# Block products: which of two accumulators is copied out before the third sum

## The chip, the cores and the metric

The kernel runs on one core of a Trainium2 chip. What counts is the device time of one execution, in microseconds (us). Of the kernel before, three runs gave 2841.8, 5434.66 and 2838.23 us, so the median is 2841.8 us. TensorE is called PE below (PEld is its weight load), VectorE is DVE, ScalarE is ACT, GpSimd is POOL and SyncE is SP.

## The reference

One transformer block over 2048 rows of width 1024, in float32: an RMSNorm and one input projection, two groups of attention heads, an output projection with a residual add, a second RMSNorm and a gated FFN of width 2816, and a last norm. The change touches only the products in the first and the last of these stages:

```python
h = rmsnorm(x, norm1_g[l])
proj = jnp.einsum('bsd,de->bse', h, w_in[l])
dq, dk, dv, fq, fk, fv, fg = jnp.split(proj, SPLITS, axis=-1)
...
h2 = rmsnorm(x, norm2_g[l])
g = jnp.einsum('bsd,df->bsf', h2, w_gate[l])
u = jnp.einsum('bsd,df->bsf', h2, w_up[l])
x = x + jnp.einsum('bsf,fd->bsd', jax.nn.silu(g) * u, w_down[l])
```

## The kernel before

The large matrix products are cut into two by two blocks and computed with seven block products (P1 to P7) in place of eight, as Strassen and Winograd do it. In the input projection the class `Features` does this for a pair of 128 output features, in the FFN the class `Matrix` does it for one gate or one up matrix (11 of each for each half of the rows, so 44 matrices; in the trace each of them has three matmul lines, L1393 to L1395, and those of `Features` have L434 to L436). One product is twelve matmuls of 128x128 by 128x512: four slices of the inner dimension, and for each slice three matmuls, because every float32 operand is split into a high part (a cast on ACT, L159) and a low part (a subtraction on DVE, L160).

The products of one matrix are computed in the order P1, P2, P6, P5, P7, P3, P4. They go to three banks of PSUM: A takes P1, then P6, P7 and P4 are accumulated on top; B takes P5 and then P3; C takes P2. After a product its method `take` reads the bank. With (i, j) for the four output blocks this gives

- (0, 0): a copy of A after P1 (ACT), plus C after P2 (DVE, L1408 or L449)
- (0, 1): a copy of A after P6 (ACT), plus B after P3 (DVE, L1411 or L452)
- (1, 1): a copy of A after P7 (ACT, L1403 or L444), plus B, which then holds P5 alone (DVE, L1405 or L446)
- (1, 0): A after P4, read where it lies

A product that accumulates on a bank cannot start before the readers of that bank are done. So P3 (bank B) waits for the DVE sum of (1, 1), and P4 (bank A) waits for the ACT copy after P7. In the FFN `done` then applies the silu (ACT, L1422) or multiplies gate by up (DVE, L1426), and `activations` forms sums of the results (DVE, L1440 to L1448) in a ring of three buffers named t, which POOL stores to DRAM (a_d, L1435). In the first half of the rows the same ring and DVE also make the sums of blocks of w_down (L1346, reading tiles wd, stored as wd_d by POOL, L1461).

A scheduler of the framework sets the order of the instructions on each engine from its own cost model. Each engine then runs its list strictly in that order. Beside the products, the first part of the input projection also loads further rows of x (SP, L209), squares them (ACT, L217), forms the reciprocal root (POOL, L218 and L137 to L138), scales the rows (ACT, L221), and transposes them (PE, L246). The later part computes the forget gates (ACT L709 to L711 with table loads, a DVE scan in L716).

Of the kernel before, what the change touches and what calls it, by code (L numbers as in the profile page):

```python
# [59 lines left out]
def block_kernel(  # L60
# [21 lines left out]
    nc = tc.nc  # L82
# [79 lines left out]
    with ExitStack() as c1:  # L162
# [32 lines left out]
        def ut(name="u"):  # L195
            return up.tile([P, 512], F32, name=name, tag="u")
# [194 lines left out]
        class Features:  # L391
# [46 lines left out]
            def take(self, p):  # L438

                acc, d = self.bank[BANK_OF[p]], self.dst  # L440
                if p in ("P1", "P6", "P7"):
                    i = dict(P1=(0, 0), P6=(0, 1), P7=(1, 1))[p]
                    d[i] = ut()
                    nc.scalar.copy(d[i], acc)  # L444
                    if p == "P7":
                        nc.vector.tensor_add(d[1, 1], self.bank["B"], d[1, 1])  # L446
                        self.done(1, 1)
                elif p == "P2":
                    nc.vector.tensor_add(d[0, 0], acc, d[0, 0])  # L449
                    self.done(0, 0)  # L450
                elif p == "P3":
                    nc.vector.tensor_add(d[0, 1], acc, d[0, 1])  # L452
                    self.done(0, 1)
                elif p == "P4":
                    d[1, 0] = acc
                    self.done(1, 0)
# [864 lines left out]
    with ExitStack() as c4:  # L1321
# [9 lines left out]
        def t2(ring, name):  # L1331
            return rings[ring].tile([P, 512], F32, name=name, tag=ring)
# [25 lines left out]
        class Matrix:  # L1358
# [38 lines left out]
            def take(self, p):  # L1397

                acc, d = self.bank[BANK_OF[p]], self.dst
                if p in ("P1", "P6", "P7"):  # L1400
                    i = dict(P1=(0, 0), P6=(0, 1), P7=(1, 1))[p]
                    d[i] = t2("u" if self.up else "g", "u")
                    nc.scalar.copy(d[i], acc)  # L1403
                    if p == "P7":
                        nc.vector.tensor_add(d[1, 1], self.bank["B"], d[1, 1])  # L1405
                        self.done(1, 1)
                elif p == "P2":
                    nc.vector.tensor_add(d[0, 0], acc, d[0, 0])  # L1408
                    self.done(0, 0)
                elif p == "P3":  # L1410
                    nc.vector.tensor_add(d[0, 1], acc, d[0, 1])  # L1411
                    self.done(0, 1)
                elif p == "P4":
                    d[1, 0] = acc
                    self.done(1, 0)
# [351 lines left out]
```

## Time and profile before

| | |
|---|---|
| median of three runs | 2841.8 us |
| the profiled execution, and its span | 2842.74 us, 2840.9 us |
| PE busy in the span | 2753.1 us, 97% |
| DVE, ACT, POOL busy | 1910.0 us, 1502.0 us, 629.8 us |
| granted clock from 1546 to 1995 us, FFN's first half | 1.00 |
| granted clock from 93 to 200 us, input projection | 0.90 |

The span is the profiled execution from its first to its last instruction. A matmul of 512 columns is shown with 0.39 us although the next one starts some 0.23 us later: matmuls overlap in the pipeline, and so a stall of PE is best read from the starts of two neighbours, not from the idle time alone. The granted clock is the share of 2.4 GHz that TensorE was given.

### The profile page before, as it was taken

To read this page: it belongs to the slowest core of one execution; us is meant where nothing else is said; L and a number is where in the kernel's file an instruction comes from. 1 tells how busy PE (TensorE), PEld (TensorE's weight loads), DVE (VectorE), ACT (ScalarE), POOL (GpSimd) and SP (SyncE) were. 2 spreads that over 40 slices of the span, in tenths; PEclk is the share of its full clock that TensorE was granted. 3 is DMA by queue.
4 is the path that set the end of the run, shared out by engine and by line. 5 is a ranking of instruction groups with operands and counts; after the bars stand their busy time and mean duration, and the time that the engine had idled before them with its cause. 6 is when DMAs were issued, how large, how long until landed. Compare 5 with 4: busy or idle time off the path is not lost.

```text
span 2840.9 us, 40678 instructions
## 1 busy us (share of the span) xinstructions
PE 2753.1 (97%) x13950; PEld 2282.7 (80%) x13950; DVE 1910.0 (67%) x3788; ACT 1502.0 (53%) x3004; POOL 629.8 (22%) x1125
## 2 busy tenths in 40 slices
PE   7989999999999999999999999999999999999998
PEld 6777878789989887877877777787888788888886
DVE  7767456688898888886254766665777666665555
ACT  6545444477887888886344333333555333333444
POOL 3342012434334333332121111111001000110001
PEclk9999999999999999999999999999999999999999
DMA  7887544754423332324465544445776333334664
GB/s 259 288 286 271 182 158 149 223 116 141 132 75 108 96 97 78 96 80 150 157 228 181 175 165 159 163 145 183 244 238 213 115 108 101 104 111 154 216 201 163
DMA packets 177808, 462.39 MB, mean 163 GB/s; under 512 B 27152, under 2 KB 43680, under 8 KB 177600
## 3 DMA queue, kind: packets, MB, share of 16 engines
q1 hardware_dynamic: 130336, 319.64, 36.1%
q0 software_dynamic: 47232, 140.14, 13.8%
q8 instruction: 110, 1.80, 0.3%
q14 instruction: 98, 0.80, 0.1%
q10 hardware_dynamic: 32, 0.01, 0.0%
HBM read 311.14 MB, written 148.44 MB: 162 GB/s over the span
## 4 chain that ended last, share of the span: by engine, by line
PE 67%; issue 18%; POOL 4%; DMA 4%; ACT 4%; DVE 3%; SPq 0%; POOLq 0%; DVEq 0%; ACTq 0%
PE ps L1056 6%; PE psF L1393 6%; PE psF L1394 6%; PE psF L1395 6%; PE psF L1513 4%; PE psF L1512 4%; PE psF L1511 4%; PE psS L899 4%; PE psS L900 4%; PE psO L991 3%; PE psO L985 2%; PE psO L984 2%; PE psF L434 2%; PE psF L436 2%; PE psF L435 2%
## 5 line engine op out<-in xcount | busy, mean ns | idle before, releaser
L1393 PE MATMUL psF<-hhP,wop 128*128 128x512 f32 x1232 | 478.4, 394 | 13.4 <-DVE u L1405 10.9
L1394 PE MATMUL psF<-hlP,wop 128*128 128x512 f32 x1232 | 480.7, 390 | 0.0
L1395 PE MATMUL psF<-hhP,wop 128*128 128x512 f32 x1232 | 479.6, 390 | 0.0
L929 ACT ACTIVATE p_sb<-p_sb,mx 128x1024 f32<-128x1024 f32 (+7 forms) x384 | 343.6, 901 | 26.8 <-DVE mx L910 19.3
L1393 PEld LDWEIGHTS psF<-hhP,wop 128*128 128x128 f32 x1232 | 231.5, 188 | 79.4 <-DVE u L1405 22.1
L899 PE MATMUL psS<-ks,q 128*128 128x512 f32 (+2 forms) x640 | 272.8, 426 | 6.5 <-DVE mx L916 4.2
L1395 PEld LDWEIGHTS psF<-hhP,wop 128*128 128x128 f32 x1232 | 231.7, 188 | 49.1 <-DVE wop L160 0.2
L1394 PEld LDWEIGHTS psF<-hlP,wop 128*128 128x128 f32 x1232 | 231.8, 188 | 44.8
L1056 PE MATMUL ps<-ident,p_sb 128*128 128x128 f32 x1632 | 253.2, 276 | 9.5 <-ACT thd L1082 5.3
L159 ACT CAST wop<-sP 128x512 fp32r<-128x512 f32 x228 | 141.4, 622 | 228.6 <-PE psF L1395 186.3
L1512 PE MATMUL psF<-dop 128*128 128x512 f32 x616 | 239.7, 389 | 1.5 <-DVE dop L160 1.5
L1511 PE MATMUL psF<-dop 128*128 128x512 f32 x616 | 239.6, 389 | 0.0
L1513 PE MATMUL psF<-dop 128*128 128x512 f32 x616 | 239.6, 389 | 0.0
L900 PE MATMUL psS<-ks,q 128*128 128x512 f32 (+2 forms) x640 | 233.9, 366 | 0.0
L1056 PEld LDWEIGHTS ps<-ident,p_sb 128*128 128x128 f32 x1632 | 196.1, 142 | 41.3 <-ACT thd L1082 7.5
L160 DVE TENSOR_TENSOR wop<-sP,wop 128x512 fp32r<-128x512 f32 x228 | 156.6, 688 | 95.0 <-ACT wop L159 94.5
L159 ACT CAST dop<-wr 128x512 fp32r<-128x512 f32 x154 | 95.8, 622 | 203.9 <-PE psF L1513 190.6
L160 DVE TENSOR_TENSOR dop<-wr,dop 128x512 fp32r<-128x512 f32 x154 | 106.1, 689 | 133.3 <-ACT dop L159 132.8
L1403 ACT COPY u<-psF 128x512 f32<-128x512 f32 x132 | 77.7, 589 | 197.6 <-PE psF L1395 197.6
L142 DVE TENSOR_TENSOR th<-ps,th 128x512 fp32r<-128x512 f32 (+1 forms) x232 | 146.9, 650 | 32.3 <-ACT th L141 31.4
L1435 POOL DMA_DIRECT2D a_d<-u x88 | 47.7, 542 | 533.0 <-DVE u L1426 527.9
L434 PE MATMUL psF<-phP,wop 128*128 128x512 f32 x364 | 147.3, 409 | 13.5 <-ACT u L444 10.5
(264 smaller groups left out, 6434.1 us busy)
## 6 DMA issues: line engine op xcount, KB each, us to landing
ar<-a_d SPq DMA_DIRECT2D x70, 512.0 KB, 4.0
wr<-in_w_gate_dram SPq DMA_DIRECT2D x44, 512.0 KB, 4.5
wr<-in_w_up_dram SPq DMA_DIRECT2D x44, 512.0 KB, 5.3
a_d<-u POOLq DMA_DIRECT2D x88, 256.0 KB, 3.5
wr<-wd_d SPq DMA_DIRECT2D x40, 512.0 KB, 4.3
we<-in_w_e_dram SPq DMA_DIRECT2D x38, 512.0 KB, 4.4
a_d<-t POOLq DMA_DIRECT2D x66, 256.0 KB, 2.8
q<-fq_d SPq DMA_DIRECT2D x64, 256.0 KB, 4.0
```

Of the source, the lines that this page charges most:

```text
L159: nc.scalar.copy(hi, src)
L160: nc.vector.tensor_sub(lo, src, f32(hi))
L899: nc.tensor.matmul(pm[:, 0:mw], q[:, m, 0, qc], ks[:, m, cols], start=True, stop=False)
L900: nc.tensor.matmul(pm[:, 0:mw], q[:, m, 1, qc], ks[:, m, cols], start=False, stop=not last)
L929: nc.scalar.activation(pv, pv, AF.Exp, scale=-1.0, bias=st[m], accum_out=acc)
L1056: nc.tensor.transpose(ps[:, (2 * i + s) * P:(2 * i + s + 1) * P], p_of(u, s, m, k0 + i), ident)
L1393: nc.tensor.matmul(acc, o[:, 0, ks_], hh[:, k, :], start=first and k == 0, stop=False, **go)
L1394: nc.tensor.matmul(acc, o[:, 0, ks_], hl[:, k, :], start=False, stop=False, **go)
L1395: nc.tensor.matmul(acc, o[:, 1, ks_], hh[:, k, :], start=False, stop=k == 3, **go)
L1511: nc.tensor.matmul(acc, a[:, 0, bs], w[:, 0, :], start=first and m == 0, stop=False, **go)
L1512: nc.tensor.matmul(acc, a[:, 0, bs], w[:, 1, :], start=False, stop=False, **go)
L1513: nc.tensor.matmul(acc, a[:, 1, bs], w[:, 0, :], start=False, stop=m == NF // 2 - 1, **go)
```

## The change

In both classes the copy into the buffer of (1, 1) is now made after P5, from bank B. After P7 DVE adds bank A itself to that copy. The counts of copies and sums stay the same. The buffer of (1, 1) is taken from its ring one product earlier. P3 now waits for an ACT copy that can start when P5 ends, and P4 waits for the DVE sum that can start when P7 ends.

```diff
@@ in class Features (input projection) and class Matrix (FFN) @@
-                if p in ("P1", "P6", "P7"):
-                    i = dict(P1=(0, 0), P6=(0, 1), P7=(1, 1))[p]
+                if p in ("P1", "P6", "P5"):
+                    i = dict(P1=(0, 0), P6=(0, 1), P5=(1, 1))[p]
                     d[i] = ut()
                     nc.scalar.copy(d[i], acc)
-                    if p == "P7":
-                        nc.vector.tensor_add(d[1, 1], self.bank["B"], d[1, 1])
-                        self.done(1, 1)
+                elif p == "P7":
+                    nc.vector.tensor_add(d[1, 1], acc, d[1, 1])
+                    self.done(1, 1)
```

The scheduler makes other lists of it. Two places follow, with two engines each.

PE in the FFN, where the fifth of seven products ends (P7, bank psF_19914, with B in psF_19973 and the next matrix's A in psF_20060). Before:

```order
L1395 MATMUL psF_19914<-hhP7_17302,wop_19931 128x512
L1393 MATMUL psF_20060<-hhP1_15691,wop_19992 128x512
L1394 MATMUL psF_20060<-hlP1_15692,wop_19992 128x512
L1395 MATMUL psF_20060<-hhP1_15691,wop_19992 128x512
L1393 MATMUL psF_20060<-hhP1_15691,wop_19992 128x512
L1393 MATMUL psF_19914<-hhP4_17306,wop_19970 128x512
L1394 MATMUL psF_19914<-hlP4_17307,wop_19970 128x512
L1395 MATMUL psF_19914<-hhP4_17306,wop_19970 128x512
L1393 MATMUL psF_19973<-hhP3_17304,wop_19951 128x512
```

After:

```order
L1395 MATMUL psF_19914<-hhP7_17302,wop_19931 128x512
L1393 MATMUL psF_19973<-hhP3_17304,wop_19951 128x512
L1394 MATMUL psF_19973<-hlP3_17305,wop_19951 128x512
L1395 MATMUL psF_19973<-hhP3_17304,wop_19951 128x512
...
L1393 MATMUL psF_19914<-hhP4_17306,wop_19970 128x512
L1394 MATMUL psF_19914<-hlP4_17307,wop_19970 128x512
L1395 MATMUL psF_19914<-hhP4_17306,wop_19970 128x512
...
L1393 MATMUL psF_20060<-hhP1_15691,wop_19994 128x512
```

Before, four matmuls of the next matrix and three of P4 stand between P7 and P3. After, P3 and P4 follow whole, and the next matrix starts behind them. So P3 and P4 of a matrix end seven and four matmuls earlier than before.

DVE in the FFN's first half, from the end of an up matrix into the next gate (L1426 with psF is the product with block (1, 0), L1440 to L1448 are the sums in t, sP are the sums of weight blocks, wop low parts of weights, L1408 is the sum for (0, 0) of the gate):

```order
-L1426 TENSOR_TENSOR u<-u,psF 128x512
 L1447 TENSOR_TENSOR t<-u,t 128x512
 L1448 TENSOR_TENSOR u<-u 128x512
+L1426 TENSOR_TENSOR u<-u,psF 128x512
 L1346 TENSOR_TENSOR sP_19230<-wd 128x512
 L160 TENSOR_TENSOR wop<-wr,wop 128x512
-L1346 TENSOR_TENSOR sP_19251<-sP_19230,wd 128x512
-L160 TENSOR_TENSOR wop<-wr,wop 128x512
-L1408 TENSOR_TENSOR u<-psF,u 128x512
+L1346 TENSOR_TENSOR sP_19253<-sP_19230,wd 128x512
 L1440 TENSOR_TENSOR t<-u,t 128x512
```

L1440, the last sum of a gate and up pair, now stands ahead of L1408 instead of behind it.

PE in the input projection, in the first pair of features (phP_144 is the operand of P7, phP_146 that of P3, phP_1074 that of P4 and phP_136 that of P1; L246 are the transposes of rows of x):

```order
 L435 MATMUL psF<-plP_145,wop 128x512
 L436 MATMUL psF<-phP_144,wop 128x512
-L246 MATMUL psF<-ident,xt 128x128 x8
-L434 MATMUL psF<-phP_136,wop 128x512
-L434 MATMUL psF<-phP_1074,wop 128x512
-L435 MATMUL psF<-plP_1075,wop 128x512
-L436 MATMUL psF<-phP_1074,wop 128x512
 L434 MATMUL psF<-phP_146,wop 128x512
 L435 MATMUL psF<-plP_147,wop 128x512
```

The transposes, and the pieces of P1 and P4, no longer stand between P7 and P3; the transposes come after P4.

ACT in the same pair of features (L217 squares rows of x, L221 scales them, L444 is the copy out of a bank):

```order
 L217 ACTIVATE psF,s_1134<-xt 128x512 x2
-L159 CAST wop<-we 128x512
+L444 COPY u<-psF 128x512
 L221 ACTIVATE xt<-xt,rstd 128x512 x4
-L444 COPY u<-psF 128x512
+L159 CAST wop<-we 128x512
+L159 CAST hl<-u 128x512
 L159 CAST wop<-we 128x512
```

The copy for (1, 1) stood behind the four scalings and now stands ahead of them.

## Rows read from the trace of the kernel before

**Rows 1.** The page, busy time of each engine, share, instructions.

```profile
PE 2753.1 (97%) x13950; PEld 2282.7 (80%) x13950; DVE 1910.0 (67%) x3788; ACT 1502.0 (53%) x3004; POOL 629.8 (22%) x1125
```

**Rows 2.** Windows: stretch, its length, busy times by engine, PEclk, DMA share, GB/s.

```profile
93.00:200.00 107.00, 93.58 (x397) 74.86 (x396) 68.70 (x112) 57.11 (x121) 51.73 (x93) 0.90 0.82 275
...
1546.00:1995.00 449.00, 438.80 (x1913) 355.17 (x1913) 294.68 (x457) 169.20 (x288) 68.47 (x126) 1.00 0.51 171
```

**Rows 3.** Timeline, PE: start, duration, instruction, idle and releaser; undisturbed matmuls.

```profile
1712.18 0.39 PE L1395 MATMUL psF<-hhP,wop 128*128 128x512 f32 x1
...
1721.02 0.39 PE L1395 MATMUL psF<-hhP,wop 128*128 128x512 f32 x1
```

**Rows 4.** Timeline of a gate in the FFN's first half, around P7's end.

```profile
1724.76 0.50 PE L1393 MATMUL psF<-hhP,wop 128*128 128x512 f32 x1 [1.02 <-DVE u L1405]
1725.09 0.39 PE L1394 MATMUL psF<-hlP,wop 128*128 128x512 f32 x1
...
1721.48 0.69 DVE L1346 TENSOR_TENSOR sP<-wd,sP 128x512 f32<-128x512 f32 x1 [0.71 <-DMA a_d<-t]
...
1724.02 0.68 DVE L1405 TENSOR_TENSOR u<-psF,u 128x512 f32<-128x512 f32 x1
...
1722.13 0.59 ACT L1403 COPY u<-psF 128x512 f32<-128x512 f32 x1 [2.04 <-PE psF L1395]
```

**Rows 5.** Timeline, PE: the same place in other matrices, and the down projection's start.

```profile
1606.92 0.50 PE L1393 MATMUL psF<-hhP,wop 128*128 128x512 f32 x1 [1.24 <-DVE u L1405]
...
1922.45 0.50 PE L1393 MATMUL psF<-hhP,wop 128*128 128x512 f32 x1 [1.16 <-DVE u L1405]
...
1996.70 0.50 PE L1512 MATMUL psF<-dop 128*128 128x512 f32 x1 [1.49 <-DVE dop L160]
...
2211.97 0.50 PE L1393 MATMUL psF<-hhP,wop 128*128 128x512 f32 x1 [1.15 <-DVE u L1405]
...
2230.52 0.40 PE L1394 MATMUL psF<-hlP,wop 128*128 128x512 f32 x1
...
2287.99 0.40 PE L1394 MATMUL psF<-hlP,wop 128*128 128x512 f32 x1
```

**Rows 6.** Timeline, PE, input projection: transposes at full clock, then P7's end.

```profile
22.22 1.91 PE L246 MATMUL psF<-ident,xt 128*128 128x128 f32 x16
...
106.82 0.39 PE L436 MATMUL psF<-phP,wop 128*128 128x512 f32 x1
...
113.58 0.40 PE L435 MATMUL psF<-plP,wop 128*128 128x512 f32 x1
```

**Rows 7.** Timeline, ACT, at the same place.

```profile
107.34 2.56 ACT L221 ACTIVATE xt<-xt,rstd 128x512 f32<-128x512 f32 x4 [1.32 <-POOL rstd L138]
109.81 0.56 ACT L444 COPY u<-psF 128x512 f32<-128x512 f32 x1
```

**Rows 8.** Timeline, PE, three other places behind P7.

```profile
164.52 1.30 PE L246 MATMUL psF<-ident,xt 128*128 128x128 f32 x4 [1.92 <-ACT xt L221]
...
408.06 0.80 PE L434 MATMUL psF<-phP,wop 128*128 128x512 f32 x1 [2.96 <-DVE u L446]
...
413.78 0.46 PE L434 MATMUL psF<-phP,wop 128*128 128x512 f32 x1
...
544.15 0.50 PE L434 MATMUL psF<-phP,wop 128*128 128x512 f32 x1 [0.73 <-ACT u L444]
```

**Rows 9.** Timeline, PE and ACT: stalls at the copies after P6 and P1.

```profile
129.49 0.50 PE L434 MATMUL psF<-phP,wop 128*128 128x512 f32 x1 [3.04 <-ACT u L444]
...
183.31 0.79 PE L434 MATMUL psF<-phP,wop 128*128 128x512 f32 x1 [4.03 <-ACT u L444]
...
179.47 0.60 ACT L217 ACTIVATE psF<-xt 128x512 f32<-128x512 f32 x1 [5.98 <-DMA xt<-in_x_dram]
```

**Rows 10.** Timeline, DVE, FFN's first half: the sum for (0, 1) of an up matrix.

```profile
1707.40 0.69 DVE L1411 TENSOR_TENSOR u<-psF,u 128x512 f32<-128x512 f32 x1 [1.31 <-PE psF L1395]
```

**Rows 11.** Tile t in the FFN's first half: who waited for its stores (us, times).

```profile
  DVE sP L1346: 14.9, 10
```

More of the change, by code (lines that the diff above doesn't have):

```diff
@@ L1399, in take @@
                 acc, d = self.bank[BANK_OF[p]], self.dst
-                if p in ("P1", "P6", "P7"):
-                    i = dict(P1=(0, 0), P6=(0, 1), P7=(1, 1))[p]
+                if p in ("P1", "P6", "P5"):
+                    i = dict(P1=(0, 0), P6=(0, 1), P5=(1, 1))[p]
                     d[i] = t2("u" if self.up else "g", "u")
                     nc.scalar.copy(d[i], acc)
-                    if p == "P7":
-                        nc.vector.tensor_add(d[1, 1], self.bank["B"], d[1, 1])
-                        self.done(1, 1)
+                elif p == "P7":
+                    nc.vector.tensor_add(d[1, 1], acc, d[1, 1])
+                    self.done(1, 1)
                 elif p == "P2":
```

## The prediction

> **What bounds the kernel now.** I read the page's busy times first, then the windows, then PE's timeline, and last the timelines of the engines that PE waits for. PE is busy for 2753.1 of 2840.9 us, 97% [rows 1]; the next, DVE, has 67%. So a microsecond is won only where PE stalls or runs slowly, and a gain on DVE or ACT by itself is worth nothing. The windows tell where that is: in the FFN's first half the clock is 1.00 and PE is idle for 449.0 − 438.8 = 10.2 us; in the input projection from 93 to 200 us it is idle for 13.4 of 107 us and the clock is only 0.90 [rows 2].
>
> The unit of the sums is the step from one matmul's start to the next. Between 1712.18 and 1721.02 us stand 39 undisturbed matmuls: 8.84 / 39 = 0.2267 us [rows 3]. One product (12 matmuls) is 2.72 us, one matrix (84) 19.04 us. A stall is what a stretch takes beyond that.
>
> **The FFN's first half.** The row at 1724.76 is P3's first matmul, idle for 1.02 us until the DVE sum L1405 [rows 4]. P7 had ended by 1722.13, when ACT's copy starts behind it; the sum stood on DVE from 1724.02 to 1724.70. The same place is at 1606.92 and, eight gate and up pairs later, at 1922.45 [rows 5]: 315.53 / 8 = 39.44 us a pair, where 168 × 0.2267 = 38.08 are needed. That is 1.36 us a pair. Ten of the eleven gates show it: **13.6 us**.
>
> After the change P3 waits for a copy of bank B that can start when P5 ends; P7 lies between, 2.72 us. ACT had been idle for 2.04 us ahead of the copy [rows 4], a copy takes 0.59, so P3 should find its bank free. P4 now waits for L1405, and P3 lies between: again 2.72 us. Before, the sum ended 1724.70 − 1722.13 = 2.6 us after P7. That alone would just do. It should come sooner, because DVE's list starts sooner: in the up matrix before, L1411 waits 1.31 us for P3 [rows 10], and P3 now ends seven matmuls, 1.6 us, earlier. L1440, whose store to DRAM is waited for, also moves ahead of L1408. I estimate that the sum ends 1.0 to 2.0 us after P7, with no stall left. The copy is as long from bank B as from A, and the sum as long with A as with B: cost nothing.
>
> The removed cover matters too. P1's four matmuls and P4's three, 7 × 0.2267 = 1.6 us, no longer stand between P7 and P3. They are still executed, so PE's work is the same; what they covered is what the copy after P5 no longer needs covered.
>
> **The down projection's start and the second half.** At 1996.70 the down projection starts after 1.49 us of idle time [rows 5]: DVE's low part of its operand is late, while matmuls of P4 had been spent already. After, P3 and P4 stand ahead of it: 1.8 us with the slower first matmuls. In the second half the first gate, at 2211.97, loses 1.4 us. From 2230.52 to 2287.99 three matrices take 57.47 us, 19.157 each, so 0.11 us over 19.04; for 21 matrices that is 2.4 us. Together **5.6 us**. For the FFN that is 19.2; I leave 1.2 as residue (eleven gates, 0.1 us each) and take **18 us**.
>
> What a pause does to the clock. In the FFN the matmul after the gate's pause, at 1725.09, follows 0.33 us behind 1724.76 [rows 4], and the window has the clock at 1.00 [rows 2]: a pause of about 1 us costs its own length. At 408.06 in the input projection PE had idled 2.96 us, and from there to 413.78 its 13 matmuls take 5.72 us in place of 2.95 [rows 8]: PE ran at the lower of its two levels for most of it, and the pause cost 2.96 + 2.77 = 5.7 us.
> The Trainium skill, "TensorE: Matmul & The Clock Gate", section "HAM oscillation — how this bites in real kernels", says that a loop whose pauses let the clock fall pays half speed again behind every pause; applied to the ten gates it would give about 27 us in place of 13.6, and 2798 us in all. The clock of 1.00 speaks against that in the FFN; the input projection's row agrees with it.
>
> **The input projection.** Four places behind P7 are long.
> - At 106.82 P7 ends, and at 113.58 PE is back at its rate [rows 6]: 6.76 us for nine matmuls and eight transposes, which need 9 × 0.2267 + 8 × 1.91 / 16 = 3.0. ACT's copy L444 stands behind four scalings L221 that waited for the reciprocal root until 107.34, and comes at 109.81 [rows 7]. The order now has the copy ahead of them, P3 and P4 straight behind P7, and the transposes after. Gain 3.8.
> - At 164.52 PE waits 1.92 us for L221, again for transposes put between P7 and P3 [rows 8]. With as much again for the clock, as at 408.06: 3.6. Bounds: 0, if the later transposes meet the same late rows of x, and 3.6; I take 3.6, because P3 and P4, 5.4 us of work, now stand ahead of them.
> - At 408.06: 5.7. The sum L446 stays late (the scan is ahead of it on DVE), and now holds P4: P3 covers 2.72 of the idle 2.96, and I leave 0.5. Gain 5.2.
> - At 544.15: 0.73 [rows 8].
>
> The other eight pairs gain 0.1 each as in the FFN: 0.8. Sum 14.1. At 129.49 P7 waits for the copy after P6, at 183.31 a product waits for the copy after P1 [rows 9]; the change leaves both. Work that reaches them earlier may wait longer there for rows of x, since L217 at 179.47 waited 5.98 us for a load [rows 9]: I take off 1. **13 us**, between 0 and 21.
>
> **The sum.** 18 + 13 = 31. The profiled execution took 2842.7 us, 0.9 above the median of the runs: 2842.7 − 31 = 2811.7, or 2811 from the median. I forecast 2811. Attention and output projection keep their lists; instruction counts stay the same.
>
> **The rivals.**
> 1. *Only the FFN gains.* The input projection between 93 and 200 us moves at 275 GB/s with DMA engines 0.82 busy [rows 2], and the loads of x end its waits [rows 9]. If they set the end there, a stall removed behind P7 comes back at the next row of x. Against it: the scan's place (408.06) and 107 us are not behind a load of x. 2842.7 − 18 = 2825.
> 2. *The other copies gain too.* If P1's and P6's copies also come earlier, the pauses of 3.04 and 4.03 us [rows 9], 7.1 and as much again for the clock, go in part: 2811 − 13 = 2798. Against it: their lists on ACT do not move ahead of the scalings that hold them.
> 3. *It does not do what it says.* P4's wait takes the place of P3's, one gate as long as the other, because L1405 still ends over 2.72 us behind P7 and the cover is gone. Then only the odd places gain: about 2838.
> 4. *Slower: the store of t holds P4.* L1405 stands on DVE behind an L1346 that waits for the store of t, 14.9 us in 10 waits [rows 11], 0.71 of them at 1721.48 [rows 4]. It decides from the point where the sum ends 2.72 us behind P7; before it had 0.1 us to spare. If with shorter pairs the store landed 3 us later, each gate would stop for 2.9 us, and such a pause brings the slow clock, 2.8 more [rows 8]: ten times 5.7 = 57, so 2811 + 57 = 2868. Against it: L1440 now comes earlier, and so does all of DVE's list from L1411 on.
> The Trainium skill, same page, section "Architectural detail: the array is 16× 32×32, not 1× 128×128", says that DVE and ACT take their queue strictly in order, on which this rival hangs; the traces agree, since L1405 follows the waiting L1346 in the list.
>
> **How the numbers follow.** Forecast (2803 to 2821) 0.58; rival 1 0.20; rival 2 0.10; rival 3 0.07; rival 4 0.05. The forecast's own bounds are the input projection's 13 against 21, and a residue of up to 0.5 us in each gate or 0.3 in each place of the input projection. To leave out no more than 2 in 10 the range reaches to rival 1 above and nearly to rival 2 below: 2799 to 2830. A measurement of this kernel tells about 2% from no change, which is 57 us: faster begins at 2785, slower at 2899. No case lies beyond either; I give 0.02 to each for the tails of rivals 2 and 4, and 0.96 to no change by that bound.
>
> **What the next profile would show.** Right: in the FFN no idle time ahead of P3 for L1405, pairs of 38.1 us, the clock still 1.00; P4's first matmul with no wait on DVE; P3 straight behind P7 at about 107 us; some 0.5 us of wait for L446 near 400 us; the pauses of [rows 9] still there. Wrong: a wait for L1405 ahead of P4 (rivals 3 and 4), with slow matmuls behind it (4); the pause at 129.49 or 183.31 longer by what 107 and 165 us gave back (1), or gone (2). What I know least is how DVE's waits for stores shift when pairs shorten, and how the loads of x bind the early input projection.

## The result, and the profile after

The changed kernel takes 2815.3 us (median of four runs, 2812.9 to 2817.9) against 2843.4 us for the kernel before on the same chip. One of the four runs of the kernel before took 5434.66 us and is not in the ratio, 0.991, with a 95% interval of 0.990 to 0.992: 0.9% faster, some 26 us by the ratio and 28 by the medians. The forecast was 2811 us, in a range of 2799 to 2830. The profiled execution took 2814.8 us with a span of 2813.0, so 27.9 us less than the span before.

By stage, from the first matmul of one to the first of the next, the input projection became 12.0 us shorter (attention's first matmul at 540.02 instead of 551.99), attention and output projection 0.9, and the FFN 15.0 (1279.5 instead of 1294.5). Forecast were 13, 0 and 18.

The page first. PE's busy time falls by 16.6 us against [rows 1], at the same number of instructions. Part of that is the clock, as the windows below show; the rest was not taken apart.

```profile
PE 2736.5 (97%) x13950; PEld 2285.3 (81%) x13950; DVE 1917.6 (68%) x3788; ACT 1500.8 (53%) x3004; POOL 629.2 (22%) x1125
```

The windows of the two stretches of [rows 2], the second from the new start of the FFN and as long as before (columns as there):

```profile
93.00:200.00 107.00, 95.64 (x421) 77.26 (x421) 70.21 (x114) 59.96 (x126) 53.01 (x97) 0.94 0.86 297
1533.00:1982.00 449.00, 445.41 (x1957) 368.17 (x1958) 307.42 (x470) 174.01 (x296) 68.99 (x127) 0.99 0.53 178
```

In the FFN's first half PE was idle for 10.2 us and is now for 3.6, with 44 more matmuls in the same time. In the input projection the clock rose from 0.90 to 0.94 only, and the DMA engines are busier, 0.86 against 0.82.

Who waited for the tiles u (that is, for the copies and sums of the FFN), before from 1546 to 1995 us:

```profile
  PE psF L1393: 9.8, 10
```

and after from 1533 to 1982 us (us in total, times):

```profile
  PE psF L1393: 1.9, 1
```

Ten waits became one. The gate of [rows 4] after the change, on DVE (start, duration, instruction, idle time and what ended it), with the sum of an earlier gate ahead of it:

```profile
1594.14 0.69 DVE L1405 TENSOR_TENSOR u<-psF,u 128x512 f32<-128x512 f32 x1 [0.16 <-PE psF L1395]
...
1704.89 0.69 DVE L1346 TENSOR_TENSOR sP<-wd,sP 128x512 f32<-128x512 f32 x1 [0.25 <-DMA a_d<-t]
...
1708.38 0.69 DVE L1405 TENSOR_TENSOR u<-psF,u 128x512 f32<-128x512 f32 x1
...
1711.10 0.69 DVE L1411 TENSOR_TENSOR u<-psF,u 128x512 f32<-128x512 f32 x1 [0.59 <-PE psF L1395]
```

At 1594.14 DVE sits ready and is released by P7's end. The sum takes 0.69 us, so it ends 0.7 us after P7, where [rows 4] had 2.6. P3 covers 2.72, so the sum is done 1.8 us before P4's turn at 1596.66. The wait for the store of t ahead of it is 0.25 us where it was 0.71. Over the first half the waits for these stores, 14.9 us in [rows 11], fell (1533 to 1982 us; total, times):

```profile
  DVE sP L1346: 3.1, 6
```

The one wait that is left stands in the first gate. PE, then DVE:

```profile
1555.14 0.50 PE L1395 MATMUL psF<-hhP,wop 128*128 128x512 f32 x1 [1.15 <-DVE wop L160]
1557.55 0.76 PE L1393 MATMUL psF<-hhP,wop 128*128 128x512 f32 x1 [1.91 <-DVE u L1405]
...
1558.53 0.63 PE L1395 MATMUL psF<-hhP,wop 128*128 128x512 f32 x1
```

```profile
1553.79 0.69 DVE L1346 TENSOR_TENSOR sP<-wr 128x512 f32<-128x512 f32 x1 [2.01 <-DMA wr<-in_w_up_dram]
...
1556.81 0.68 DVE L1405 TENSOR_TENSOR u<-psF,u 128x512 f32<-128x512 f32 x1
```

The sum that P4 needs stands on DVE behind weight sums, the first of which waited 2.01 us for the first load of w_up. With the slow matmuls behind it, steps of 0.43 us, this gate loses 5.2 us; before, the same gate lost 1.6 at P3.

In the input projection, the place of [rows 6] is gone: the transposes run together, after P4, with no wait. What follows is not, on PE and ACT:

```profile
112.55 1.04 PE L246 MATMUL psF<-ident,xt 128*128 128x128 f32 x8
...
128.67 0.79 PE L434 MATMUL psF<-phP,wop 128*128 128x512 f32 x1 [5.99 <-ACT u L444]
...
401.98 0.50 PE L434 MATMUL psF<-phP,wop 128*128 128x512 f32 x1 [1.90 <-DVE u L446]
```

```profile
122.09 0.60 ACT L217 ACTIVATE psF<-xt 128x512 f32<-128x512 f32 x1 [1.42 <-DMA xt<-in_x_dram]
...
126.82 1.33 ACT L221 ACTIVATE xt<-xt,rstd 128x512 f32<-128x512 f32 x2 [1.55 <-POOL rstd L138]
128.06 0.56 ACT L444 COPY u<-psF 128x512 f32<-128x512 f32 x1
```

This is the place of [rows 9] at 129.49. It waited 3.04 us then and 5.99 now, and starts only 0.8 us sooner, although PE had been some 4 us ahead. The copy after P6 stands on ACT behind scalings, these behind the reciprocal root on POOL, and that, in this execution, behind rows of x for which ACT waited 1.42 us. The late rows are not the whole of it: in a second execution of the same kernel (e5r_after) ACT found x without a wait, and PE still waited 5.11 us (rows under "x ahead of the weights"). The wait for the sum L446 is 1.90 us in place of 2.96 [rows 8], and no slow matmuls follow it.

The pause at 183.31 [rows 9], which was to stay, is gone; near it there are shorter waits of 0.68, 0.51 and 1.65 us, the last two for scaled rows. The first matmul of the value projection has the same 420 matmuls of feature pairs ahead of it in both kernels. It divides the 12.0 us: 5.4 had been won there, the other 6.6 behind it. Before, then after:

```profile
227.95 0.39 PE L493 MATMUL psF<-wop,phP 128*128 128x512 f32 x1
```

```profile
222.53 0.39 PE L493 MATMUL psF<-wop,phP 128*128 128x512 f32 x1
```

### The profile page after: what moved, and what is told of

It reads as the page before. It is cut to its first block, busy times and chain, and to the rows that moved or that the text cites. A ratio compares the mean times of both kernels' runs of the same rounds, so it can differ in the third digit from the quotient of the medians.

```text
span 2813.0 us, 40683 instructions
## 1 busy us (share of the span) xinstructions
PE 2736.5 (97%) x13950; PEld 2285.3 (81%) x13950; DVE 1917.6 (68%) x3788; ACT 1500.8 (53%) x3004; POOL 629.2 (22%) x1125
## 4 chain that ended last, share of the span: by engine, by line
PE 84%; ACT 4%; DMA 4%; issue 3%; DVE 2%; POOL 2%; SPq 0%; POOLq 0%; DVEq 0%; ACTq 0%
PE psF L1393 10%; PE psF L1394 10%; PE psF L1395 10%; PE ps L1056 6%; PE psF L1511 5%; PE psF L1513 5%; PE psF L1512 5%; PE psS L899 4%; PE psS L900 4%; PE psO L991 3%; PE psO L985 2%; PE psO L984 2%; PE psF L434 2%; PE psF L435 2%; PE psF L436 2%
## 5 line engine op out<-in xcount | busy, mean ns | idle before, releaser
L1393 PE MATMUL psF<-hhP,wop 128*128 128x512 f32 x1232 | 481.1, 390 | 4.4 <-DVE hlP L160 2.5
L1393 PEld LDWEIGHTS psF<-hhP,wop 128*128 128x128 f32 x1232 | 232.0, 188 | 53.8 <-ACT wop L159 3.1
L984 PE MATMUL psO<-th,v 128*128 128x256 f32 x544 | 159.2, 317 | 1.6 <-DMA v<-fv_d 1.0
```

What stands on the lines that cost most here:

```text
L1393: nc.tensor.matmul(acc, o[:, 0, ks_], hh[:, k, :], start=first and k == 0, stop=False, **go)
```

## The experiments

Each was timed beside the kernel before; ratios are to that, with 95% intervals (its median lay between 2838.2 and 2843.4 us in the different sets, so the ratios compare better than the medians). The stage marks are read from the profiles: the first matmul of attention and of the FFN, and from the latter to the end of the span. Each profile is one execution; that of e2 took 2837.0 us, 8 above its median.

| kernel | ratio | median us | attention starts | FFN starts | FFN, us |
|---|---|---|---|---|---|
| before | 1 | 2843.4 | 551.99 | 1546.41 | 1294.5 |
| changed | 0.9908 (0.9897 to 0.9920) | 2815.3 | 540.02 | 1533.53 | 1279.5 |
| changed, again (e5r_after) | 0.9901 (0.9885 to 0.9917) | 2811.7 | 540.17 | 1533.43 | 1279.2 |
| e1_ffn_only | 0.9933 (0.9919 to 0.9947) | 2821.4 | 549.92 | 1541.99 | 1276.1 |
| e2_ip_only | 0.9963 (0.9950 to 0.9977) | 2829.1 | 543.32 | 1535.52 | 1299.7 |
| e3_wd_later | 0.9888 (0.9874 to 0.9902) | 2810.1 | 546.30 | 1536.76 | 1274.2 |
| e4_p6_dve | 0.9899 (0.9882 to 0.9915) | 2811.1 | 536.83 | 1529.90 | 1279.1 |
| e5_both | 0.9887 (0.9872 to 0.9902) | 2808.6 | 539.39 | 1533.09 | 1274.1 |
| e7_after_6more | 0.9990 (0.9980 to 1.0001) | 2838.0 | 545.00 | 1540.26 | 1298.6 |
| e8_before_2more | 0.9973 (0.9963 to 0.9983) | 2833.2 | 551.28 | 1544.93 | 1287.7 |
| e9_x_first | 0.9896 (0.9882 to 0.9910) | 2810.1 | 539.93 | 1530.65 | 1278.9 |
| e10_all | 0.9906 (0.9892 to 0.9921) | 2813.3 | 548.76 | 1536.79 | 1274.0 |

**One half of the change at a time.** e1 keeps the old `take` in `Features`, e2 keeps it in `Matrix`.

```diff
 # e1_ffn_only: class Features as before, class Matrix as changed; e2_ip_only: the other way round
-                if p in ("P1", "P6", "P7"):
+                if p in ("P1", "P6", "P5"):
```

> The change in the FFN alone. Theory 1 (stalls behind P7 are local, the two halves of the change add up): the FFN became 15.0 us shorter between the two traces (1294.5 to 1279.5), so 2843.4 - 15 = 2828, ratio 0.995, the first gate still with some 5 us of stall. Rival (the input projection's gain and the FFN's depend on each other, for example through transfers that arrive earlier): outside 2825 to 2832, with a first gate that does not stall as in the changed kernel.

> The change in the input projection alone. Theory 1 (additive): 12.0 us came back before the attention starts (551.99 to 540.02), so 2843.4 - 12 = 2831, ratio 0.996, and the FFN with its ten waits of P3 for the sum. Rival (the input projection's gain is an accident of its loads of x): over 2836 or under 2826.

e1 took 0.67% off, some 19 us, e2 0.37%, some 10.5. Together 1.04%, the change 0.92%: they add up within their intervals, but the FFN's share is larger, and the other smaller, than the one pair of profiles had said. So e2 came as expected and e1 did not: 2821.4 us lies below the 2825 to 2832, and 0.995 outside its interval. The rival had a first gate without a stall; it still waits in e1, but alone and with the clock at 1.00 behind it, and the FFN is 3 us shorter than in the changed kernel:

```profile
1564.76 0.50 PE L1393 MATMUL psF<-hhP,wop 128*128 128x512 f32 x1 [1.90 <-DVE u L1405]
```

In e2, on PE, P7 of the input projection waits near 130 us as in the changed kernel, and the gates wait as before:

```profile
130.37 0.80 PE L434 MATMUL psF<-phP,wop 128*128 128x512 f32 x1 [6.87 <-ACT u L444]
...
1599.00 0.50 PE L1393 MATMUL psF<-hhP,wop 128*128 128x512 f32 x1 [1.19 <-DVE u L1405]
```

The table shows why the pair misled. With the old input projection attention starts at 549.9 to 552.0 us (before, e1, e8: mean 551.1), with the changed one at 540.0 to 546.3 (changed twice, e2, e3, e7: mean 543.0). So the gain there is about 8 us, and the wait behind P6's copy near 130 us varies in these five from 5.1 to 9.9. The FFN takes 1294.5 and 1299.7 us by the old way (before, e2), 1276.1 to 1279.5 by the new (changed twice, e1, e4, e9: mean 1278.6), about 18 us less. By the same marks the value projection starts at 226.9 us in the mean of the three and 224.2 of the five, so 2.7 of the 8 us are won ahead of it, where the five differ by 3.6 us, and some 5 behind it.

**The first gate.** In e3 the loads and sums of w_down of the first gate begin later, so that w_up's first load is issued ahead of them.

```diff
-                    if s[2] == "P2":
+                    if s[2] == ("P2" if s[1].n else "P5"):
                         wd = down_sums(s[1].n)
-                    if s[2] != "P1":
+                    if s[2] != "P1" and at > 2:
+                        next(wd, None)
+                    if at == 6:
                         next(wd, None)
```

> The changed kernel, with the first gate's loads and sums of w_down begun at P5 in place of P2, so that the first loads of w_up stand ahead of those of w_down in the queue of SP and in the ring of raw tiles. Theory 1 (the first gate's new stall of 5.1 us is the sum L1405 queued on DVE behind a weight sum that waits 2.0 us for the first w_up): that load comes 3 us or more earlier, the stall goes to under 1 us, and the time from 2815.3 to 2811 (2809 to 2812.5). Rival (DVE's list itself is late there, whatever the load does): 2814 to 2816, the wait for L1405 still above 1.5 us.

The load was issued 5 us after the FFN's start where it had been 12.5 (1546.05 in the changed kernel), on SP's queue:

```profile
1541.71 1.79 SPq L1370 DMA_DIRECT2D wr<-in_w_up_dram  x2
```

From the FFN's start to 2000 us no matmul of the gates waits for DVE any more; the 2.5 us in the group of L1393 (busy time, mean, idle time before) are the wait at the FFN's start itself:

```profile
L1393 PE MATMUL psF<-hhP,wop 128*128 128x512 f32 x616 | 240.6, 391 | 2.5 <-DVE hlP L160 2.5
```

The FFN took 1274.2 us, 5 less, as again in e5 and e10 (1274.1, 1274.0). So the new stall came from that load, through DVE's list; the rival is refuted. The time of the whole kernel, as expected at 2810.1, cannot show it as clearly: its interval overlaps that of the changed kernel. In the profiled execution the input projection, the same in both, ended 6 us later, at 546.30.

**P6's copy on DVE.** In e4 it no longer stands behind the scalings on ACT.

```diff
                     d[i] = ut()
-                    nc.scalar.copy(d[i], acc)
+                    if p == "P6":
+                        nc.vector.tensor_copy(d[i], acc)
+                    else:
+                        nc.scalar.copy(d[i], acc)
```

> The changed kernel, with P6's copy out of the bank on DVE in place of ACT, in the input projection alone. Theory 1 (P7 waits 6.0 us at 128.67 because that copy stands on ACT behind scalings that wait for the reciprocal root; what the change gave at 107 us was lost there): the wait goes, the transposes wait later for the same rows of x, and about half of the 9 us (6.0 idle, 3 at the lower clock) stays won: 2811 (2806 to 2813). Rival (the loads of x set the end of that stretch, so the wait only moves): 2814 to 2816.

```profile
123.69 0.50 PE L434 MATMUL psF<-phP,wop 128*128 128x512 f32 x1 [1.22 <-DVE u L445]
...
150.80 0.50 PE L434 MATMUL psF<-phP,wop 128*128 128x512 f32 x1 [3.22 <-DVE u L445]
...
176.36 0.33 PE L246 MATMUL psF<-ident,xt 128*128 128x128 f32 x1 [1.80 <-ACT xt L221]
```

The wait of 5.99 became 1.22, but PE waits 3.22 for the next copy after P6, where the changed kernel had 0.76 and 1.35, and the transposes at 176 wait for scaled rows, as they did there. Attention starts at 536.83, 3 us before the earliest of the changed kernel; the time, as expected at 2811.1, is not told apart from it (0.9899 against 0.9901 and 0.9908).

**x ahead of the weights.** In e9 the value projection's weights (wv) are taken up at other steps, so that the second pair of rows of x is loaded ahead of the second wv.

```diff
-                    if at % 2:
+                    if at in (1, 3, 5, 7) or at > 10 and at % 2 == 0:
                         next(bg[1], None)
```

> The changed kernel, with the second to the last of the value projection's weight loads (wv, with their sums and stores) taken up at other steps of the first feature pairs, so that the second pair's rows of x are loaded ahead of the second wv. Theory (in four runs with this input projection P6's copy near 130 us came 6 to 7 us after the rows of x had landed, and these landed 9.7 to 11.6 us after an issue that stands behind wv): x lands 2 to 3 us earlier, the wait behind P6's copy falls from 5 to 10 us to 2 to 5, and the attention starts at 537 to 541 in place of 540 to 546; 2809 (2806 to 2813). Rival (the reciprocal root on POOL, behind wv's stores, or the ACT list sets it, not the landing): the wait stays at 5 us or more, 2811 to 2816.

ACT found x at 120.41 without a wait, and PE's wait near 130 us was gone altogether. But the edit did more than bring x: in ACT's list the copy after P6 now stands ahead of the scalings. ACT in e9, then in the changed kernel's second run, where x was on hand as early, the copy stood behind the scalings, and PE waited 5.11 us:

```profile
122.79 0.56 ACT L444 COPY u<-psF 128x512 f32<-128x512 f32 x1
...
125.94 2.56 ACT L221 ACTIVATE xt<-xt,rstd 128x512 f32<-128x512 f32 x4 [1.45 <-POOL rstd L138]
```

```profile
120.51 0.60 ACT L217 ACTIVATE psF<-xt 128x512 f32<-128x512 f32 x1
...
125.85 1.33 ACT L221 ACTIVATE xt<-xt,rstd 128x512 f32<-128x512 f32 x2 [1.56 <-POOL rstd L138]
127.09 0.56 ACT L444 COPY u<-psF 128x512 f32<-128x512 f32 x1
```

So the place in ACT's list, which the rival named, is enough to hold the copy; that x's landing alone does is not shown. PE's waits after that in e9:

```profile
149.01 0.79 PE L434 MATMUL psF<-phP,wop 128*128 128x512 f32 x1 [2.45 <-ACT u L444]
...
166.11 0.50 PE L434 MATMUL psF<-phP,wop 128*128 128x512 f32 x1 [1.86 <-ACT u L444]
...
176.51 0.33 PE L246 MATMUL psF<-ident,xt 128*128 128x128 f32 x1 [1.95 <-ACT xt L221]
...
190.91 0.50 PE L434 MATMUL psF<-phP,wop 128*128 128x512 f32 x1 [2.99 <-DVE u L446]
```

The time and attention's start lie in the expected ranges, but the gain was not there: attention starts at 539.93, where the changed kernel had 540.02 and 540.17. These four waits are 9.3 us, where the changed kernel had 2.0 and 4.9 at the same places: most of what one place gave came back at others. That the supply of rows and weights sets the pace from 93 to 200 us fits this, but no run shows it.

**Both edits, and all three.** e5 has the edits of e3 and e4, e10 that of e9 as well; with the changed kernel beside e5.

> The two edits that shortened the changed kernel put together: w_down's first loads and sums from P5 on, and P6's copy of the input projection on DVE. They touch different stages, so their gains should add: 5 us in the FFN's first gate and 4 in the input projection, 2806 (2803 to 2809), ratio to the kernel before 0.987. Rival (the input projection's end moves with its loads of x from run to run, and the 4 us were that): 2810, as with the first edit alone.

> The changed kernel once more, beside the kernel with both edits on the same chip. Theory (its input projection varies with the landing of x and of the v weights, 9.7 to 11.6 us after the issue): the wait behind P6's copy near 130 us between 5 and 10 us long; the FFN again with a stall at the first gate alone; the time 2813 to 2818.

> All three edits together: w_down's first loads later, P6's copy of the input projection on DVE, and x ahead of the second wv. Theory: the first gate does not stall, and the wait behind P6's copy is under 1 us near 125 us: 2804 (2801 to 2808). Rival (what is left in the input projection is the later transposes' wait for x, which only moves): 2807 to 2810, as without the third edit.

e5 has the lowest median, 2808.6 against 2811.7 for the changed kernel beside it, but their intervals overlap; what repeats, in e3, e5 and e10, is the 5 us in the FFN's marks. The changed kernel itself came out at 2811.7, below the 2813 to 2818 expected. e10 was expected to be best and is not: 2813.3 lies above its range and the rival's. The first gate is right (1274.0), and attention starts at 548.76. Its DVE carries the copies and its x comes in another order, and the transposes at 182.73 wait 5.99 us for the scaling; 4.38 us more are a wait of attention's first matmul for its loads (1.70 in the changed kernel). What sets the input projection's end there was not followed further.

**How much cover is enough?** e7 lengthens the way from P7 to P4 on DVE in the changed kernel, e8 the way from P7 to P3 in the kernel before.

```diff
 # e7_after_6more
                     nc.vector.tensor_add(d[1, 1], acc, d[1, 1])
+                    for _ in range(3):
+                        nc.vector.tensor_add(d[1, 1], acc, d[1, 1])
+                        nc.vector.tensor_sub(d[1, 1], d[1, 1], acc)
                     self.done(1, 1)
 # e8_before_2more
                         nc.vector.tensor_add(d[1, 1], self.bank["B"], d[1, 1])
+                        nc.vector.tensor_add(d[1, 1], self.bank["B"], d[1, 1])
+                        nc.vector.tensor_sub(d[1, 1], d[1, 1], self.bank["B"])
```

> The changed kernel with six more DVE operations on each of the FFN's 44 blocks (1, 1), between P7 and P4's start: the bank is added and taken away again three times over, 0.6 us each. The scheduler answers with more cover: after P3 come 12 matmuls of the next P1 and two or three of P2 ahead of P4, 2.7 + 3.3 = 6.0 us after P7 in place of 2.7. Theory (what decides is only whether the sum ends inside the cover): it ends 0.9 + 3.6 = 4.5 us after P7, no stall, 2815 (2813 to 2822), though DVE has 160 us more to do. Rival (DVE's lateness moves on to the weight sums and the next products): 2840 or more.

> The kernel before, with two more DVE operations on each of the FFN's 44 blocks (1, 1): bank B is added and taken away once more behind the sum, so that P3 is released 1.2 us later. The scheduler answers by placing all of P4 and six matmuls of P1 between P7 and P3, 18 matmuls or 4.1 us in place of 7 or 1.6. Theory (the FFN's waits of P3 came from too short a cover, not from too much work): the sum now ends 2.6 + 1.2 = 3.8 us after P7, inside 4.1, and the kernel becomes faster in spite of 88 added operations: 2830 (2826 to 2835). Rival (the later release costs what it costs): ten to eleven gates lose another 0.5 to 1.2 us each, 2848 to 2860.

e7 missed: 2838.0 us, 0.999 of the kernel before, where the theory had 2815 and the rival 2840 or more. The FFN lost 19 us to the changed kernel. DVE, then PE, in the first half:

```profile
1683.21 0.68 DVE L1405 TENSOR_TENSOR u<-psF,u 128x512 f32<-128x512 f32 x1
...
1690.41 0.68 DVE L1408 TENSOR_TENSOR u<-u,psF 128x512 f32<-128x512 f32 x1
```

```profile
1691.14 0.50 PE L1393 MATMUL psF<-hhP,wop 128*128 128x512 f32 x1 [1.20 <-DVE u L1408]
```

The first sum and the six more end only 7.9 us after the first began, not 4.2: other work of DVE's list stands between any two of them. So they did not end inside the cover of 6 us, and P4 waits for the very last of them. A wait where the sum ends outside its cover is what the theory says; that it would end inside was a wrong reckoning of DVE: with DVE's list full, each added operation costs two places in it, and that is the lateness of which the rival spoke. In the second half, where DVE is freer, no such wait is left.

e8 became faster with 88 operations more, 0.27% or 7.7 us, inside the range of the theory and not of the rival. The FFN took 1287.7. What is left, the group of L1393 from 1568 to 1995 us (PE) and one wait of DVE:

```profile
L1393 PE MATMUL psF<-hhP,wop 128*128 128x512 f32 x587 | 227.2, 393 | 7.0 <-DVE u L1407 7.0
```

```profile
1912.23 0.69 DVE L1346 TENSOR_TENSOR sP<-wd 128x512 f32<-128x512 f32 x1 [3.64 <-DMA wd_d<-sP]
```

P3 still waits for the sum, 7.0 us in six gates of the first half (9.8 in ten before), so the sum did not end inside the cover everywhere; at 1918.44, where it waits 2.19, DVE's list had been held by a store (3.64 us here). But longer cover, given by the scheduler in answer to more work, was worth more than the work cost. So how many matmuls stand between weighed more in the waits of P3 than DVE's time.

## Why the prediction was right, and where not

- *PE is the bound, and a stall counts only there*: right. DVE's busy time rose by 7.6 us while the kernel became 28 us faster.
- *FFN, first half: no wait ahead of P3, the sum 1.0 to 2.0 us after P7, P4 on time*: right for ten of eleven gates. The sum came even earlier, 0.7 us after P7 where DVE is free. Rivals 3 and 4 need that sum later than 2.72 us; they are refuted there.
- *The first gate*: missed. I took all eleven gates for the same. In the first, the mechanism of rival 4 is real, with a load of w_up in place of the store of t. The gate loses 5.2 us where it lost 1.6, and the residue of 1.2 was too small for that: it is more than the 3 us by which the FFN's 15.0 fell short of 18. e3 shows its cause.
- *Down projection's start and second half, 5.6*: right. No pause over 0.2 us is left there, and with equal matmuls counted these stretches became 5.2 us shorter.
- *FFN 18*: 15.0 in the two profiles, about 18 in the mean of seven, 19 by e1's time.
- *Input projection 13*: 12.0 in the pair, about 8 by the means. The term was too large, and in the pair it came near by luck, since its parts were off both ways. At 107 us the transposes wait no more, as forecast. The step that failed most is "I take off 1": at 129.49 the wait grew from 3.04 to 5.99 and ate most of the 3.8. At 164.52, taken for 3.6, the transposes still wait, 0.79 and 0.90 us, and the clock still falls (0.73 from 162.4 to 168). Against that, "the change leaves both" was wrong in the kernel's favour: the 4.03 us at 183.31 are gone; why stays open. Of the signs of being wrong, that of rival 1 came at 129.49 and that of rival 2 at 183.31. But the copy at 129.49 is held by its place in ACT's list too, and not by rows of x alone, as rival 1 had it.
- *408.06, gain 5.2 with 0.5 us left*: 1.90 us are left, in all five executions with the new input projection. P3's 2.72 us were taken off a wait of 2.96 that had cover already: nine matmuls, 2.0 us, stood between P7 and P3. P3 adds only 0.7 to that. Most of what is won here is the slow clock, which does not follow the shorter pause.
- *The clock*: in the FFN a pause of about 1 us cost its own length, as the rows said, and the gain of 15 to 19 us fits the 18 forecast from rows. The Trainium skill, "TensorE: Matmul & The Clock Gate", section "HAM oscillation — how this bites in real kernels", is about pauses long enough for the clock to fall. Those of the ten gates were not, with the clock at 1.00 [rows 2], so the 27 us worked out from it never applied to them.

## What to carry to other kernels

Where a product must wait for a reader of its bank, count the matmuls between the release's start and the waiting product, and move the read to the accumulator that is needed last; e8 shows that longer cover can pay even with more work. What a wait still costs is net of the cover it has: longer cover takes off only the difference. A gain read at one stall is worth that much only if nothing downstream waits on the same lists: in the stretch where DMA was 0.86 busy it came back in part at the next copy, so follow the next two waits before adding it up. And look at the first round of a loop by itself, since its loads can be late in a way that the others' are not, as here that of w_up.

## What the runs showed of the hardware

Matmuls came 0.43 us apart behind some pauses and 0.23 behind others. The first is the lower of the clock's two levels: from 408.0 to 413.8 us of the kernel before, in the place of [rows 8], the granted clock was 0.50. A single pause of about 2 us left the clock up in the FFN: 1.90 us at 1564.76 in e1, 2.09 at 1850.75 in e7, 2.19 at 1918.44 and 2.20 at 1570.62 in e8. The granted clock of the 3.3 to 3.4 us behind each was 1.00, and so it was behind the 1.90 us at 401.98 in the changed kernel. Where another pause stood one to three matmuls ahead, it fell: to 0.53 over 3.6 us behind 1.91 at 1557.55 in the changed kernel (1.15 ahead of it), to 0.66 behind 1.90 at 1556.63 in its second run (0.33 ahead), to 0.60 behind 2.08 at 1610.74 in e7 (1.62 ahead). At 1557.55 the slow matmuls added 1.7 us. In the input projection it also fell behind pauses without another so close: 0.73 over 6 us behind 2.45 at 149.01 in e9, 0.77 over 7.5 us behind 1.92 at 164.52 before. So two pauses close together cost more in the FFN than a longer one alone; nothing was run to test it.

POOL's reciprocal root took 1.91 us in both runs of the changed kernel, in e2 and in e3; two rows of POOL and the last two of DVE's list at that time:

```profile
124.23 1.91 POOL L137 TENSOR_SCALAR rstd<-ss 128x1 f32<-128x1 f32 x1
...
130.23 0.19 POOL L137 TENSOR_SCALAR rstd<-ss 128x1 f32<-128x1 f32 x1
```

```profile
124.81 0.69 DVE L541 TENSOR_TENSOR wv<-wv 128x512 f32<-128x512 f32 x1
125.41 0.69 DVE L160 TENSOR_TENSOR hl<-u,hl 128x512 fp32r<-128x512 f32 x1
```

The same instruction takes 0.19 us at 130.23 and 1.91 at 124.23, where it ends at 126.14, just as DVE's run of operations with two SBUF operands ends at 126.10. The Trainium skill, "SBUF — State Buffer", section "SBUF: two separate sides", says that DVE and GpSimd take turns at one pair of ports and that the loser is held for whole instructions. The rows agree with that; no run here tested it.
